# Border to the feed-forward part: operands made product by product, the cross output's second half by rows, the last transposes behind products

## The chip, the core and the metric

One core of a Trainium2 chip runs the kernel. The metric is the device time of one execution in microseconds (us): 1808.42 as the median of three runs (1808.24 to 1808.46). The engines are TensorE (PE), VectorE (DVE), ScalarE (ACT) and GpSimd (POOL); SyncE (SP) issues the transfers. Each engine runs its own instructions in a fixed order and waits where an operand or a buffer is not ready.

## The reference

One layer on 1024 tokens of width 1024, all in float32: an attention part, a cross attention to 256 memory tokens, and a gated feed-forward part. The change touches the seam between the last two:

```
x = x + memory_cross_attention(hc, mn, w_cq, w_ckv, w_co)   # ends in o @ w_co
hf = rmsnorm(x, norm_ffn_g)
g, u = split(hf @ w_gate_up, 2)                             # width 2 x 2816
x = x + (silu(g) * u) @ w_down
out = rmsnorm(x, norm_final_g)
```

## The kernel before

**Three matmuls for one product.** Every float32 operand is split in two halves: `hi` is a cast on ScalarE, `lo = src - hi` a subtraction on VectorE. A product is hi*hi + lo*hi + hi*lo, so three matmuls (`prod`, L887 to L889 in the feed-forward part). Neither half can be made before the operand is there, and the matmul at L888 needs the weight's `lo`.

**End of the cross attention.** The output weights come as eight units of 512 KB (`unit`, L82), each loaded into one of two `raw` buffers and split into one of three `wsp` buffers. A step (`out_steps`, L626) multiplies one block of 128 rows with two units, twelve matmuls, and VectorE adds the result to the residual `xs` (L632), which frees one of two accumulators. Eight row blocks times two halves of columns (`cc`) make sixteen steps. Four jobs hold them (`last_job`, L795): first the row blocks 0 to 3, `cc` 0 and then 1, then the row blocks 4 to 7, all four for `cc` 0 and then all four for `cc` 1. When a row block has both halves, `rms` normalises it: a square on ScalarE (L106), two small steps on GpSimd (L99, L101), a scaling on VectorE (L108). Then `norms` transposes it on TensorE (L789), and ScalarE and VectorE copy the result to `hq` (L792). The last rows' transposes stand before the first feed-forward product.

**Feed-forward products.** Gate and up are done with a scheme of seven products instead of eight: operands of rows 0 to 3 (`b11`, `b21`) and of rows 4 to 7 (`b12`, `b22`) and differences of them. `T[n]` is the split operand of product kind n, `w` the split weight. The order of the kinds is 1, 2, 6, 5, 7, 3, 4. Kinds 1 and 2 need rows 0 to 3 alone; their operands are made in `mov_early`, all others in `mov_late` (L906), four 1024-wide differences on VectorE, four on GpSimd (L914, L917), ten splits. A tile is two 128-wide column blocks of gate and two of up. The products of the first two tiles are ordered so that kinds 1 and 2 of both come first: products 0 to 3 are kinds 1 and 2 of the first tile (gate, up, gate, up), 4 to 7 those of the second tile, and 8 on the kinds 6, 5, 7, 3, 4 of the first tile. `run` (L1062) makes each weight four products ahead (`AHEAD`), and calls `mov_late` at product 1. For kinds 6 and 3 the weights are differences made on GpSimd (L942 to L946). `down_weights` (L1027) makes differences of the down weights of the same tile on GpSimd, after its first product.

**What sets the order.** A scheduler puts the recorded instructions in an order for each engine; within an engine this order is fixed in the built program. The buffers of the weights `fr` are those of the residual `xs`: the loads of the up weights of the first and the second tile wait until the rows 4, 5 and 6, 7 are stored (L804).

## Time and profile before

| what | value |
|---|---|
| time, median of three runs | 1808.42 us |
| profiled execution, its own time | 1810.3 us |
| span of the profiled execution | 1808.5 us |
| TensorE busy | 1746.3 us, 97% of the span |
| VectorE busy | 1102.1 us, 61% |
| ScalarE busy | 765.9 us, 42% |
| GpSimd busy | 524.5 us, 29% |

TensorE's busy time is an upper view: matmuls overlap and their ends are modelled. What a wait costs is better read from the start of one matmul to the start of the next. In the 40 slices of the span TensorE is at 9 tenths or more in all but four: the first, one in the middle at 7 tenths (the 26th, from about 1130 to 1176 us), the one behind it and the last.

### The profile page before, as it was taken

The page shows a single profiled execution, that of the slowest core. Times are in us where ns is not written, and L with a number is a line of the kernel's source. Part 1 is how long each engine was busy: PE and PEld are TensorE (multiplying, and loading weights), DVE is VectorE, ACT ScalarE, POOL GpSimd, SP SyncE. Part 2 cuts the span into 40 slices and gives each one's busy share as a digit, 9 for nine tenths or more (in the row PEclk, how much of TensorE's full clock was granted, in tenths as well). Part 3 has the DMA queues.
Part 4 walks back from the last instruction along what each step waited for, and adds up shares of the span by engine and source line. Part 5 has one row for each costly group of instructions (what it writes and reads, how often), then busy time and mean ns, then how long its engine had stood idle before and what let it go on. Part 6 is the DMA issues. An engine that isn't in the chain of part 4 may idle for free.

```text
span 1808.5 us, 23594 instructions
## 1 busy us (share of the span) xinstructions
PE 1746.3 (97%) x8836; PEld 1472.0 (81%) x8836; DVE 1102.1 (61%) x1491; ACT 765.9 (42%) x1425; POOL 524.5 (29%) x559
## 2 busy tenths in 40 slices
PE   7999999999999999999999999789999999999996
PEld 7778797898898888888888887578888888888885
DVE  6585667646756644445644546886676656655555
ACT  5354455535545544213542244443333333334343
POOL 3232213213323202200000001676666655400001
PEclk9999999999999999999999999989999999999999
DMA  5332313212222265422421123244445435586663
GB/s 191 105 88 68 103 42 102 70 53 62 78 72 68 82 233 196 151 78 71 140 82 59 47 70 140 93 151 182 180 159 190 163 140 186 205 285 195 191 194 117
DMA packets 75731, 229.81 MB, mean 127 GB/s; under 512 B 9184, under 2 KB 9440, under 8 KB 71776
## 3 DMA queue, kind: packets, MB, share of 16 engines
q1 hardware_dynamic: 75616, 228.30, 37.3%
q8 instruction: 69, 1.13, 0.3%
q14 instruction: 46, 0.38, 0.1%
HBM read 160.10 MB, written 55.57 MB: 119 GB/s over the span
## 4 chain that ended last, share of the span: by engine, by line
PE 66%; DVE 3%; issue 2%; ACT 2%; POOL 1%; DMA 0%; DVEq 0%; POOLq 0%; ACTq 0%
PE bk L888 11%; PE bk L889 11%; PE bk L887 11%; PE acc L215 5%; PE acc L216 5%; PE acc L217 5%; PE s L93 2%; PE s L94 2%; PE s L95 2%; PE s L215 2%; PE s L216 2%; PE s L217 2%; PE av L452 1%; DVE T L882 1%; PE tr L436 1%
## 5 line engine op out<-in xcount | busy, mean ns | idle before, releaser
L215 PE MATMUL acc<-t,wsp 128*128 128x512 f32 (+1 forms) x704 | 270.6, 384 | 0.0
L217 PE MATMUL acc<-t,wsp 128*128 128x512 f32 (+1 forms) x704 | 270.5, 384 | 0.0
L216 PE MATMUL acc<-t,wsp 128*128 128x512 f32 (+1 forms) x704 | 270.4, 384 | 0.0
L888 PE MATMUL bk<-T,w 128*128 128x512 f32 x616 | 241.3, 392 | 14.0 <-DVE w L882 14.0
L887 PE MATMUL bk<-T,w 128*128 128x512 f32 x616 | 241.0, 391 | 0.0
L889 PE MATMUL bk<-T,w 128*128 128x512 f32 x616 | 240.6, 391 | 0.0
L882 DVE TENSOR_TENSOR w<-fr,w 128x512 fp32r<-128x512 f32 x132 | 148.3, 1157 | 70.1 <-ACT w L881 69.8
L79 DVE TENSOR_TENSOR wsp<-raw,wsp 128x1024 fp32r<-128x1024 f32 x100 | 124.6, 1246 | 72.2 <-ACT wsp L74 71.0
L74 ACT CAST wsp<-raw 128x1024 fp32r<-128x1024 f32 x98 | 102.7, 1048 | 126.3 <-PE s L217 50.2
L217 PEld LDWEIGHTS acc<-t,wsp 128*128 128x128 f32 x704 | 133.3, 189 | 25.3
L216 PEld LDWEIGHTS acc<-t,wsp 128*128 128x128 f32 x704 | 133.3, 189 | 23.0 <-DVE wsp L79 0.7
L215 PEld LDWEIGHTS acc<-t,wsp 128*128 128x128 f32 x704 | 133.3, 189 | 22.2
L888 PEld LDWEIGHTS bk<-T,w 128*128 128x128 f32 x616 | 116.5, 189 | 39.5 <-DVE w L882 15.3
L882 DVE TENSOR_TENSOR do<-dr,do 128x1024 fp32r<-128x1024 f32 x77 | 96.8, 1260 | 82.8 <-ACT do L881 82.1
L889 PEld LDWEIGHTS bk<-T,w 128*128 128x128 f32 x616 | 116.5, 189 | 24.2
L887 PEld LDWEIGHTS bk<-T,w 128*128 128x128 f32 x616 | 116.3, 189 | 24.4 <-ACT hq L792 0.2
L881 ACT CAST do<-dr 128x1024 fp32r<-128x1024 f32 x77 | 80.9, 1050 | 118.2 <-PE bk L889 102.9
L215 PE MATMUL acc<-wsp,t 128*128 128x256 f32 (+1 forms) x384 | 124.7, 325 | 1.0 <-POOL wsp L78 1.0
L217 PE MATMUL acc<-wsp,t 128*128 128x256 f32 (+1 forms) x384 | 122.9, 320 | 1.5 <-DVE wsp L79 1.5
L216 PE MATMUL acc<-wsp,t 128*128 128x256 f32 (+1 forms) x384 | 123.0, 321 | 0.0
L888 PE MATMUL bk<-do 128*128 128x512 f32 x308 | 120.2, 390 | 1.3 <-DVE do L882 1.3
L889 PE MATMUL bk<-do 128*128 128x512 f32 x308 | 119.8, 389 | 0.0
(204 smaller groups left out, 3726.2 us busy)
## 6 DMA issues: line engine op xcount, KB each, us to landing
fr<-in_wgu SPq DMA_DIRECT2D x44, 512.0 KB, 5.2
dw<-in_wdn SPq DMA_DIRECT2D x22, 512.0 KB, 5.2
wd<-dw SPq DMA_DIRECT2D x11, 1024.0 KB, 3.9
ad<-r SPq DMA_DIRECT2D x22, 512.0 KB, 3.4
sd<-s SPq DMA_DIRECT2D x11, 1024.0 KB, 4.2
dr<-sd SPq DMA_DIRECT2D x44, 256.0 KB, 3.8
dr<-wd SPq DMA_DIRECT2D x44, 256.0 KB, 4.0
dr<-ad SPq DMA_DIRECT2D x33, 256.0 KB, 5.0
```

Source lines behind the costliest of these rows:

```text
L74: act.copy(out=hi, in_=src)
L79: lo_eng.tensor_tensor(out=lo, in0=src, in1=hi.bitcast(F32), op=ALU.subtract)
L93: pe.matmul(acc, lh, rh, start=(i == 0), stop=False)
L94: pe.matmul(acc, ll, rh, start=False, stop=False)
L215: pe.matmul(acc, lh, rh, start=(i == 0), stop=False)
L216: pe.matmul(acc, ll, rh, start=False, stop=False)
L217: pe.matmul(acc, lh, rl, start=False, stop=(i == n - 1))
L881: self.act.copy(out=hi, in_=src)
L882: self.dve.tensor_tensor(out=lo, in0=src, in1=hi.bitcast(F32), op=ALU.subtract)
L887: mm(acc, l[0], r[0], start=start, stop=False, skip_group_check=onto)
L888: mm(acc, l[1], r[0], start=False, stop=False, skip_group_check=onto)
L889: mm(acc, l[0], r[1], start=False, stop=stop, skip_group_check=onto)
```

## The change

- The second half of the cross output is no longer two jobs. `last_half` takes row block after row block, both halves of columns one after the other, with all four weight units resident: two in `wsp`, two in buffers of `t1`. Each row block is normalised and stored at once.
- `ff.before()` (early operands and the first two weights) stands behind the first step of that half.
- The last row block's transposes (`last_norm`) come behind products 0 and 1, into banks of the feed-forward part.
- `mov_late` is cut in four. The table `LATE` calls it at products 2, 7, 9 and 11 for the kinds 6 (with 5), 7, 3 and 4, and its four differences of GpSimd are VectorE's.
- The down weights of the first two tiles are made in the third and the fourth tile.

```diff
...
 LAM_INIT = 0.2
 AHEAD = 4
+LATE = {2: 6, 7: 7, 9: 3, 11: 4}
 LAG = 1
 F0, FA, FB, W0, W1 = 3, 5.5, 3.8, 0.3, 1.2
...
-    def unit(src, hi_eng=act):
+    def unit(src, hi_eng=act, home=None):
         raw = wp.tile([P, D], F32, name="raw", tag="raw", bufs=2)
         sp.dma_start(out=raw, in_=src)
-        w = wp.tile([P, 2, D], F32R, name="wsp", tag="wsp", bufs=3)
+        w = home([P, 2, D]) if home else wp.tile([P, 2, D], F32R, name="wsp", tag="wsp", bufs=3)
         split(w[:, 0], w[:, 1], raw, hi_eng, dve)
         return w
...
         hq = {}
-        def norms(n):
+        def norms(n, mk=None):
             while len(todo) > n:
                 t, xn = todo.pop(0)
                 half, o = divmod(t, 4)
                 for g in range(2):
-                    ps = (tr_tile if g == 0 else av_tile)()
+                    ps = (mk or (tr_tile if g == 0 else av_tile))()
...
-        def last_job(hh, cc):
+        def last_rms(tt):
+            xn = row_tile()
+            rms(xrow(tt), gbc, xn)
+            if tt % 2:
+                sp.dma_start(out=x_d[tt // 2], in_=xs[tt // 2])
+            todo.append((tt, xn))
+        def last_job(cc):
             def go(w):
-                for tt in range(hh * 4, hh * 4 + 4):
+                for tt in range(4):
                     yield from out_steps(o_sta(2), w, 4, cc, tt)
                     if cc == 1:
                         norms(1)
-                        xn = row_tile()
-                        rms(xrow(tt), gbc, xn)
-                        if tt % 2:
-                            sp.dma_start(out=x_d[tt // 2], in_=xs[tt // 2])
-                        todo.append((tt, xn))
-                    else:
-                        norms(0)
+                        last_rms(tt)
             return Job(Units(wco[4 + cc], wco[6 + cc]), go)
+        def last_half():
+            ws = [[unit(wco[4 + cc + 2 * i], home=t1_tile if cc else None) for i in range(2)] for cc in range(2)]
+            for tt in range(4, 8):
+                add_out(o_sta(2), ws[0], 4, 0, tt)
+                if tt == 4:
+                    norms(0)
+                    ff.before()
+                add_out(o_sta(2), ws[1], 4, 1, tt)
+                norms(0)
+                last_rms(tt)
         for h in range(4):
             u0, u1 = UnitX(h, 0), UnitX(h, 1)
...
                 feed.add(*Q[h + 1, 0])
                 feed.fill(6)
             else:
-                feed.add(last_job(0, 0))
+                feed.add(last_job(0))
                 feed.fill(8)
             u1.t()
             feed.drain()
         gbc = gain_tile(g_ffn)
-        jobs = [last_job(0, 1), last_job(1, 0), last_job(1, 1)]
-        feed.add(*jobs)
-        feed.need(*jobs[:2])
+        feed.add(last_job(1))
...
         ff = FeedForward(tc, tiles, cst, dram, hq, x_d, wgu, wdn, g_final, mhalf, out)
-        ff.before()
         feed.drain()
-        norms(0)
+        last_half()
         psctx.close()
-        ff.run()
+        ff.run(lambda: norms(0, ff.bank))
     ctx.close()
...
         for i in (0, 2):
             self.put(2, i, self.quad(i + 4, 0))
-    def mov_late(self):
-        dve, pool, sub, quad = self.dve, self.pool, ALU.subtract, self.quad
+    def mov_late(self, n):
+        dve, sub, quad = self.dve, ALU.subtract, self.quad
         for i in (0, 2):
-            b11, b12, b22 = quad(i, 0), quad(i, 1), quad(i + 4, 1)
-            dve.tensor_tensor(out=b11, in0=b12, in1=b11, op=sub)
-            self.put(5, i, b11)
-            dve.tensor_tensor(out=b11, in0=b22, in1=b11, op=sub)
-            self.put(6, i, b11)
-            pool.tensor_tensor(out=b12, in0=b22, in1=b12, op=sub)
-        for i in (0, 2):
-            b21 = quad(i + 4, 0)
-            pool.tensor_tensor(out=b21, in0=b21, in1=quad(i, 0), op=sub)
-            self.put(7, i, quad(i, 1))
-        for i in (0, 2):
-            self.put(3, i, quad(i + 4, 1))
-        for i in (0, 2):
-            self.put(4, i, quad(i + 4, 0))
+            b11, b21, b12, b22 = quad(i, 0), quad(i + 4, 0), quad(i, 1), quad(i + 4, 1)
+            if n == 6:
+                dve.tensor_tensor(out=b11, in0=b12, in1=b11, op=sub)
+                self.put(5, i, b11)
+                dve.tensor_tensor(out=b11, in0=b22, in1=b11, op=sub)
+                self.put(6, i, b11)
+            elif n == 7:
+                dve.tensor_tensor(out=b12, in0=b22, in1=b12, op=sub)
+                self.put(7, i, b12)
+            elif n == 3:
+                self.put(3, i, b22)
+            else:
+                dve.tensor_tensor(out=b21, in0=b21, in1=b11, op=sub)
+                self.put(4, i, b21)
     class Pair:
...
     class Tile2:
-        def __init__(self, ff, f):
-            self.ff, self.f = ff, f
+        def __init__(self, ff, f, before=None):
+            self.ff, self.f, self.before = ff, f, before
             self.g, self.u = ff.Pair(ff, f), ff.Pair(ff, FT + f)
             self.w = {}
...
             g, u, ff = self.g, self.u, self.ff
             if p is g:
-                if n == 1:
+                if n == 1 and self.f >= 4:
                     self.down_weights()
                 elif n == 7:
                     act.activation(g.r[1][:, 1], g.r[1][:, 1], AF.Silu)
...
+            elif n == 7 and self.before:
+                self.before.down_weights()
             elif n == 3:
                 pool.tensor_tensor(out=g.r[0], in0=g.r[0], in1=u.r[0], op=ALU.mult)
                 sp.dma_start(out=ff.a_d[self.f // 2][:, 0:2], in_=g.r[0])
...
     def before(self):
-        tiles = [self.Tile2(self, f) for f in range(0, FT, 2)]
+        tiles = []
+        for f in range(0, FT, 2):
+            tiles.append(self.Tile2(self, f, tiles[-2] if f in (4, 6) else None))
         self.items = []
         for ns, ts in ((self.ORDER[:2], tiles[:2]), (self.ORDER[2:], tiles[:2]), (self.ORDER, tiles[2:])):
             for t in ts:
...
         for i in range(2):
             self.make(i)
-    def run(self):
+    def run(self, last_norm):
         with self.tc.tile_pool(name="fps", bufs=1, space=bass.MemoryType.PSUM, reuse_waits="tile") as self.fps:
             later = []
             self.steps = [(n, j) for n in self.ORDER for j in range(FT // 2)]
...
             for i in range(2, AHEAD):
                 self.make(i)
             for i, (t, p, n) in enumerate(self.items):
-                if i == 1:
-                    self.mov_late()
+                if i == 2:
+                    last_norm()
+                if i in LATE:
+                    self.mov_late(LATE[i])
                 self.make(i + AHEAD)
                 if i == len(self.items) - 9:
                     for k in range(4):
```

In the rows of the order `xs` is the residual, `acc` an accumulator, `hq` the transposed rows, `T` a split operand, `w` a split weight from `fr` or `s1`, `r` a partial sum read from bank `bk`; numbers tell buffers apart.

VectorE before, around the early operands (kinds 1 and 2) and the steps of rows 4 to 7:

```order
L792 COPY hq_10350<-av_10437 128x4x128
L882 TENSOR_TENSOR T_10518<-hq_10343,T_10518 128x1024
L632 TENSOR_TENSOR xs_7671<-xs_7671,acc_10443 128x512
L882 TENSOR_TENSOR T_10521<-hq_10343,T_10521 128x1024
L632 TENSOR_TENSOR xs_7673<-xs_7673,acc_10457 128x512
L882 TENSOR_TENSOR T_10524<-hq_10350,T_10524 128x1024
L882 TENSOR_TENSOR T_10527<-hq_10350,T_10527 128x1024
L79 TENSOR_TENSOR wsp_10402<-raw_10400,wsp_10402 128x1024
L632 TENSOR_TENSOR xs_7673<-xs_7673,acc_10471 128x512
```

VectorE after, at the same place:

```order
L794 COPY hq_10373<-av_10470 128x4x128
L895 TENSOR_TENSOR T_10476<-hq_10366,T_10476 128x1024
L895 TENSOR_TENSOR T_10479<-hq_10366,T_10479 128x1024
L895 TENSOR_TENSOR T_10482<-hq_10373,T_10482 128x1024
L895 TENSOR_TENSOR T_10485<-hq_10373,T_10485 128x1024
L634 TENSOR_TENSOR xs_7671<-xs_7671,acc_10505 128x512
L634 TENSOR_TENSOR xs_7671<-xs_7671,acc_10527 128x512
L110 SCALAR_TENSOR_TENSOR xn_10519<-xs_7671,rstd_10524,gbc_10257 128x1024
L634 TENSOR_TENSOR xs_7671<-xs_7671,acc_10541 128x512
```

The two residual adds that stood between the four splits of `T` now stand behind all four.

VectorE before, from the low half of product 5's weight (`w_10696`) to that of product 7 (`w_10777<-fr_10542`), and the split behind it:

```order
L882 TENSOR_TENSOR w_10696<-fr_10542,w_10696 128x512
L912 TENSOR_TENSOR hq_10343<-hq_10618,hq_10343 128x1024
L882 TENSOR_TENSOR w_10777<-fr_10533,w_10777 128x512
L977 TENSOR_TENSOR r_10712<-r_10712,bk_10780 128x512
L882 TENSOR_TENSOR T_10736<-hq_10343,T_10736 128x1024
L882 TENSOR_TENSOR T_10741<-hq_10611,T_10741 128x1024
L882 TENSOR_TENSOR T_10745<-hq_10611,T_10745 128x1024
L882 TENSOR_TENSOR T_10748<-hq_10618,T_10748 128x1024
L882 TENSOR_TENSOR T_10751<-hq_10618,T_10751 128x1024
L882 TENSOR_TENSOR T_10754<-hq_10350,T_10754 128x1024
L882 TENSOR_TENSOR w_10777<-fr_10542,w_10777 128x512
L882 TENSOR_TENSOR T_10757<-hq_10350,T_10757 128x1024
```

VectorE after, from the low half of product 5's weight (`w_10684`), over those of product 6 and 7 (`w_10747`), to the first of product 8 (`w_10780`):

```order
L895 TENSOR_TENSOR w_10684<-fr_10500,w_10684 128x512
L925 TENSOR_TENSOR hq_10366<-hq_10560,hq_10366 128x1024
L895 TENSOR_TENSOR T_10732<-hq_10366,T_10732 128x1024
L895 TENSOR_TENSOR w_10747<-fr_10491,w_10747 128x512
L927 TENSOR_TENSOR hq_10366<-hq_10567,hq_10366 128x1024
L991 TENSOR_TENSOR r_10700<-r_10700,bk_10750 128x512
L895 TENSOR_TENSOR w_10747<-fr_10500,w_10747 128x512
L895 TENSOR_TENSOR T_10736<-hq_10366,T_10736 128x1024
L895 TENSOR_TENSOR T_10740<-hq_10366,T_10740 128x1024
L991 TENSOR_TENSOR r_10717<-r_10717,bk_10766 128x512
L927 TENSOR_TENSOR hq_10366<-hq_10567,hq_10366 128x1024
L895 TENSOR_TENSOR w_10780<-fr_10488,w_10780 128x512
```

Product 7's weight stood behind six splits of `T` after product 6's; now a difference and a read stand between the two, and the differences (L925, L927) and splits of kinds 5 and 6 are spread among the weights.

VectorE after, from the last operand of kind 6 (`T_10744`) over those of kind 7 (`T_10835`, `T_10839`) and 3 (`T_10873`, `T_10876`), with the weights of products 11, 12, 13 and 14:

```order
L895 TENSOR_TENSOR T_10744<-hq_10366,T_10744 128x1024
L930 TENSOR_TENSOR hq_10560<-hq_10567,hq_10560 128x1024 x2
L895 TENSOR_TENSOR w_10818<-s1_10781,w_10818 128x512
L895 TENSOR_TENSOR T_10835<-hq_10560,T_10835 128x1024
L895 TENSOR_TENSOR T_10839<-hq_10560,T_10839 128x1024
L895 TENSOR_TENSOR w_10857<-fr_10488,w_10857 128x512
L895 TENSOR_TENSOR T_10873<-hq_10567,T_10873 128x1024
L895 TENSOR_TENSOR T_10876<-hq_10567,T_10876 128x1024
L895 TENSOR_TENSOR w_10857<-fr_10497,w_10857 128x512
L895 TENSOR_TENSOR w_10894<-fr_10488,w_10894 128x512
```

The weight of product 13 (`w_10857<-fr_10497`) stands behind both operands of kind 3, which product 14 is the first to use; before, all these operands came ahead of product 7's weight.

## Rows read from the trace of the kernel before

**Rows 1.** The page's first line.
```profile
span 1808.5 us, 23594 instructions
```
**Rows 2.** TensorE's waits, 1050 to 1210 us: total us, times, longest.
```profile
PE bk L888 <- DVE w L882: 14.0, 3, 10.8
PE tr L789 <- DVE xn L108: 3.5, 3, 2.0
PE acc L217 <- DVE wsp L79: 1.5, 1, 1.5
PE av L789 <- DVE hq L792: 1.1, 1, 1.1
```
**Rows 3.** Short windows: length, busy us (count) by engine, granted clock, DMA.
```profile
1145.00:1150.00 5.00, 5.00 (x19) 4.03 (x19) 4.88 (x6) 1.76 (x3) 2.02 (x1) 0.71 0.58 213
1160.00:1165.00 5.00, 2.70 (x13) 1.90 (x12) 5.00 (x3) 0.00 (x0) 5.00 (x4) 1.00 0.00 0
1180.00:1185.00 5.00, 3.94 (x9) 3.14 (x10) 5.00 (x6) 0.92 (x2) 4.25 (x3) 0.50 0.00 0
```
**Rows 4.** TensorE's timeline at the border: start, duration, line, operation, idle before.
```profile
1112.55 0.39 PE L216 MATMUL acc<-wsp,t 128*128 128x512 f32 x1
...
1145.87 0.80 PE L887 MATMUL bk<-T,w 128*128 128x512 f32 x1
...
1152.40 0.39 PE L887 MATMUL bk<-T,w 128*128 128x512 f32 x1
...
1160.56 0.39 PE L887 MATMUL bk<-T,w 128*128 128x512 f32 x1
...
1165.87 0.39 PE L887 MATMUL bk<-T,w 128*128 128x512 f32 x1
...
1169.84 0.39 PE L887 MATMUL bk<-T,w 128*128 128x512 f32 x1
1181.06 0.79 PE L888 MATMUL bk<-T,w 128*128 128x512 f32 x1 [10.84 <-DVE w L882]
...
1185.73 0.40 PE L887 MATMUL bk<-T,w 128*128 128x512 f32 x1
```
**Rows 5.** VectorE's timeline at the border.
```profile
1111.95 1.28 DVE L108 SCALAR_TENSOR_TENSOR xn<-xs,rstd,gbc 128x1024 f32<-128x1024 f32 x1 [1.59 <-ACT wsp L74]
...
1117.42 1.28 DVE L108 SCALAR_TENSOR_TENSOR xn<-xs,rstd,gbc 128x1024 f32<-128x1024 f32 x1 [0.71 <-POOL rstd L101]
...
1140.27 0.69 DVE L882 TENSOR_TENSOR w<-fr,w 128x512 fp32r<-128x512 f32 x1
...
1146.69 2.35 DVE L910 TENSOR_TENSOR hq<-hq 128x1024 f32<-128x1024 f32 x2
...
1161.45 1.75 DVE L882 TENSOR_TENSOR w<-fr,w 128x512 fp32r<-128x512 f32 x1
...
1167.64 12.77 DVE L882 TENSOR_TENSOR T<-hq,T 128x1024 fp32r<-128x1024 f32 x6
```
**Rows 6.** ScalarE's timeline at the border.
```profile
1115.06 1.06 ACT L106 ACTIVATE xn<-xs 128x1024 f32<-128x1024 f32 x1 [1.69 <-DVE xs L632]
...
1120.13 3.90 ACT L881 CAST T<-hq 128x1024 fp32r<-128x1024 f32 x4
```
**Rows 7.** GpSimd's timeline at the border, and once beside an idle VectorE.
```profile
1147.98 6.65 POOL L914 TENSOR_TENSOR hq<-hq 128x1024 f32<-128x1024 f32 x2 [5.15 <-DVE hq L910]
...
1158.15 4.49 POOL L942 TENSOR_TENSOR s<-fr 128x512 f32<-128x512 f32 x2
...
1283.62 1.29 POOL L1034 TENSOR_TENSOR dw<-dw 128x512 f32<-128x512 f32 x1 [1.84 <-issue]
```
**Rows 8.** Transfers, 1090 to 1205 us: count, size, median us from issue to landing.
```profile
fr<-in_wgu SPq DMA_DIRECT2D x12, 512.0 KB, 4.1
xd<-xs SPq DMA_DIRECT2D x4, 1024.0 KB, 4.3
```
**Rows 9.** GpSimd's waits, 1200 to 1400 us: total us, times, longest.
```profile
POOL r L1016 <- ACT w L881: 49.6, 6, 11.1
```

## The prediction

> **What bounds the kernel now.** I read the page first: the span is 1808.5 us [rows 1], and its line on TensorE has that engine busy nearly all the time, so time can come only from the places where it stands still. The list of TensorE's waits is next: over the whole program its largest entry belongs to the border to the feed-forward part, where 20.1 us are idle in four groups, 14.0 of them on VectorE's low halves of weights [rows 2]. The table of short windows adds that the granted clock fell there twice, to 0.71 and 0.50 as means of 5 us, the lower of the two levels (1.2 instead of 2.4 GHz) for a part of them, each time after TensorE had stood still [rows 3].
>
> TensorE's timeline gives the price by start times, which is safer than idle figures. A product is twelve matmuls, and three products take 1152.40 to 1160.56, so 2.72 us each and 0.227 per matmul [rows 4]. Number the feed-forward products from 0. Product 0 starts at 1145.87, product 2 at 1152.40, product 5 at 1160.56, 6 at 1165.87, 7 at 1169.84, 8 at 1185.73 [rows 4]. From 2 to 8 that is 33.3 us for 16.3 of work: 17.0 lost. Of these the second matmul of product 7 alone waits 10.84, and the eleven gaps behind it take 4.67 instead of 2.50, 2.2 us for the clock [rows 4]. Why so late is in VectorE's timeline: a row of six splits of T, 12.77 us, stands ahead of that weight's low half [rows 5]. GpSimd works all that time [rows 7]: a step of 1024 columns takes 1.13 in a series without it (two differences in 2.35, one end overlapping) and 2.13 here, a split of 512 takes 0.69 (0.6 in a series) alone and 1.75 beside GpSimd [rows 5].
>
> **The change, part by part.** Number of matmuls, transposes, loads and casts: unchanged. Everything hangs on order. The orders are the same up to the matmul at 1112.55 [rows 4], from where I count both.
>
> *Cross output by rows.* Row block 4's second weight unit is now split behind row 2's norm, a residual add and a copy. The norm starts at 1111.95 and takes 1.28 [rows 5]; so TensorE waits 0.5 for row 2's transposes (1113.3), 0.7 for the copy that frees their second bank (1114.5), 0.9 for the split (1115.65): 2.1 where before 1.5 stood [rows 2]. Next, the early operands: before, residual adds stood between their four splits, now all four are ahead of row 4's last add (the order shows it), and that add frees one of two accumulators. The four casts on ScalarE start when row 3's transposes are copied, 1119.2 by my count, and take 3.90 [rows 6]; the last split ends at 1125.1, the add at 1125.7. TensorE would be there at 1123.15: a new wait of 2.6. Row 4's norm follows its add: 2.36 from the start of the square to that of the scaling (1115.06 to 1117.42) and 1.28 more [rows 5, 6], ready at 1129.5, one product after the add: 1.0 of wait. Rows 5 and 6 have two products behind their last add, 5.4 us against 3.6, and cost nothing; row 7 has products 0 and 1. The three waits for norms (3.5) and the copy (1.1) of before [rows 2], and the slow clock behind them, go. From 1129.5 there remain four cross products (10.9), products 0 and 1 (5.4), four rows of transposes (0.8 each) and some hand-offs: product 2 starts at 1149.3. Before it was 1152.4: 3.1 us won.
>
> *The late operands, one product at a time.* With product 2 at Z = 1149.3, VectorE has this list up to product 8: a copy, four differences and four splits of 1024, six splits of 512, two reads of PSUM. Row 7's copy waits for transposes that now stand behind product 1, and all the rest is queued behind it on VectorE: nothing starts before Z+0.7. Its third entry is a low half of the weights of product 5, which hangs on the last load: row 7's add ends at 1144.3, its store lands 4.3 later, the load that overwrites the buffer another 4.1 or somewhat more [rows 8], the cast 0.6: Z+4.8. From there on each step costs its own time, and GpSimd's eight differences of weights, which now start at 1146.8 right behind row 7's norm, get between. GpSimd's 512-wide difference takes 1.29 with VectorE idle, 2.2 beside it (4.49 for two) [rows 7]; VectorE's 512-wide split grows by 1.1. So I let the two take turns, each VectorE step from SBUF waiting out one of GpSimd's at 1.2 while there are some. The list then runs: product 6's low half at Z+12.4 (needed Z+11.1: 1.35 of wait), product 7's in time, product 8's first weight at Z+19.5 (needed Z+17.9: 1.6) and its second operand at Z+21.9 (0.8 more). Sum 3.75.
>
> Behind it GpSimd gets its buffer for the second tile's eight differences, and the turns begin anew: operands of product 12 (two splits, 2.3 each), its first weight 1.8, two splits for product 14, and only then the weight of product 13. It ends at Z+37.7; product 13 would start at Z+33.9: 3.7 of wait. Small ones at 12, 15 and 16 make 0.9 together. All of it 8.35; before, three waits of 14.0 us idle [rows 2] cost 2.59 + 1.25 + 10.99 = 14.8 by start times [rows 4], 0.28 more each, so with five larger waits I add some 1.2: 9.6 us are lost where 17.0 were.
>
> *Four differences from GpSimd to VectorE.* On GpSimd two took 6.65, on VectorE two take 2.35 [rows 5, 7], so they enter the list above at 1.13 each; GpSimd's list gets shorter by about 12 us, and its weight differences start 11 us earlier (before at 1158.15 [rows 7]).
> The Trainium skill, in "Perfetto Trace Analysis", section "Optimizing Scalar/DVE Operations", says that the two share a read port, so that moving work between them might not help. The rows agree on the contention, but not that the move is neutral: VectorE's own difference is shorter than the turn it would wait. By the page's word alone this part would be worth nothing, some 4 x (2.2 - 1.13) = 4.3 us less, 1802.3.
>
> *Down weights moved to the third and fourth tile.* Four GpSimd differences each, two loads and a store. Here they leave the crowded stretch; there GpSimd waits up to 11.1 us per tile for ScalarE's weights [rows 9], and four differences take 5.2 alone (1.29 each) and up to 9 beside VectorE [rows 7]: cost 0, and if that cover were gone, some 7 us per tile. On SP the fifth tile's weight loads come to stand behind the moved store, which waits for those differences; they are due some ten products (27 us) later, so that costs 0 too.
>
> **Sum.** 3.1 + (17.0 - 9.6) = 10.5 us. The profiled execution took 1810.3 (span 1808.5 and 1.8 around it [rows 1]): 1799.8; it lies 1.9 above the median of the runs, 1808.4, so 1798 there.
>
> Bounds. The unknown is the price of a turn. From below: if VectorE goes first everywhere, at 1.13 and 0.6, the list reaches product 8 in time and no wait is left, 9.6 less: 1788.4. From above: 2.2 per turn (GpSimd's figure beside VectorE) instead of 1.2, on some fourteen turns that count, but half of it covered by the waits already in: 7 us, 1805. I stay at 1.2, the nearest row (0.69 to 1.75).
>
> **Rivals.** *The waits vanish* (0.17): GpSimd's first eight differences run mostly while VectorE stands waiting for row 7 and for the last load, and the rest slips between. For it: VectorE has 3.4 us of idle there by my count. Against it: 17.0 us of the old profile are this very contention. 1789.
>
> *No change that counts* (0.14): TensorE's clock falls again behind the 2.6 and 3.7 us waits, at 2.2 each, and the last load lands 3 us later, which moves product 8 one for one: 10.5 - 4.4 - 3 = 3 us, 1805.3. For it: the clock fell after waits of 1.1 and 2.0 close together [rows 2, 3]. Against it: around product 5, whose wait cost 2.6, it stayed at 1.00 [rows 3, 4].
>
> *Slower* (0.07): the down weights in tiles three and four now make two sets per tile on GpSimd, the new one standing ahead of the differences for the sixth product. If the two sets together outlast GpSimd's 11.1 us of slack, the weights of the next tile come late by a set, 7 us, in both tiles: 14 us against the 10.5, 1812. It decides once less than a set's 7 us of slack is left. Against it: the 11.1 us stood there beside one set already, and TensorE has no wait on weights there.
>
> **How the numbers follow.** The forecast, 1798, has 0.62, with a range of its own from 1793 to 1803 (half a turn more or less). This measurement can tell 0.2%, 3.6 us. Faster: 0.62 + 0.17 and a little of the second rival, 0.80; the same 0.13; slower 0.07. The range takes in the first rival and the second: 1788.5 to 1806.
>
> **What would show it.** In the new profile TensorE's waits at the border should add up to some 14 us instead of 20.1, in about eight pieces, none above 4: one near 2.6 on a residual add behind four splits, one at product 8, one at product 13 for a weight behind two splits of T. Row 7's transposes should come behind product 1 without a wait. VectorE's 1024-wide steps behind them should take 1.1 to 2.4, and GpSimd's first weight difference should start right after the last norm. The down weights should add no TensorE wait in tiles three and four. The forecast is wrong if a single wait over 6 us remains, if the clock shows a stretch at the lower level for more than 5 us, or if the border has no waits at all.

## The result and the profile after

1798.74 us as the median of four runs (1796.97 to 1801.18), against 1808.44 (1808.24 to 1808.77) of the kernel before beside it: a ratio of 0.9947, 95% interval 0.9934 to 0.9959, so 9.7 us faster where 10.5 were forecast. The profiled execution is the longest of the four, 1801.2 us; its span is 9.1 us shorter than that of [rows 1]:
```profile
span 1799.4 us, 23586 instructions
```
TensorE's waits from 1050 to 1210 us (total, times, longest) answer to [rows 2]:
```profile
PE bk L900 <- ACT r L989: 5.0, 2, 2.5
PE acc L217 <- DVE xs L634: 2.5, 1, 2.5
PE bk L901 <- DVE w L895: 1.3, 1, 1.3
PE acc L219 <- DVE wsp L81: 0.7, 1, 0.7
PE av L791 <- DVE hq L794: 0.5, 1, 0.5
PE tr L791 <- ACT t L76: 0.5, 1, 0.5
PE bk L902 <- DVE T L895: 0.5, 1, 0.5
PE bk L900 <- ACT hq L794: 0.2, 1, 0.2
```
11.2 us instead of 20.1, in nine pieces, none above 2.5. The largest entry is one that the forecast did not have: ScalarE's copy of a partial sum. TensorE's timeline shows where the pieces lie (start, duration, idle before):
```profile
1125.97 0.50 PE L217 MATMUL acc<-t,t 128*128 128x512 f32 x1 [2.49 <-DVE xs L634]
...
1149.96 1.03 PE L791 MATMUL bk<-ident,xn 128*128 128x128 f32 x8
1150.75 0.48 PE L900 MATMUL bk<-T,w 128*128 128x512 f32 x1
...
1168.83 0.50 PE L901 MATMUL bk<-T,w 128*128 128x512 f32 x1 [1.27 <-DVE w L895]
1171.17 0.50 PE L902 MATMUL bk<-T,w 128*128 128x512 f32 x1 [0.45 <-DVE T L895]
...
1199.36 0.50 PE L900 MATMUL bk<-T,w 128*128 128x512 f32 x1 [2.52 <-ACT r L989]
...
1204.83 0.50 PE L900 MATMUL bk<-T,w 128*128 128x512 f32 x1 [2.43 <-ACT r L989]
```
Row 7's transposes (1149.96) stand behind product 1 and wait for nothing; product 2 starts at 1150.75; 1168.83 and 1171.17 are in product 8; 1199.36 and 1204.83 are the first matmuls of products 18 and 19. The windows for [rows 3] (granted clock third from the end):
```profile
1125.00:1130.00 5.00, 4.03 (x11) 3.20 (x12) 2.80 (x4) 1.15 (x2) 0.74 (x2) 0.69 0.00 0
1160.00:1165.00 5.00, 5.00 (x24) 4.14 (x23) 5.00 (x5) 2.01 (x3) 1.88 (x2) 1.00 0.00 0
1180.00:1185.00 5.00, 5.00 (x24) 4.14 (x23) 5.00 (x6) 3.35 (x5) 5.00 (x1) 1.00 0.00 0
1205.00:1210.00 5.00, 5.00 (x16) 3.96 (x17) 5.00 (x6) 2.32 (x6) 4.37 (x4) 0.66 0.27 108
```
The two old falls (0.71, 0.50) are gone; there are two new ones, 0.69 behind the wait of 2.49 and 0.66 behind those of 2.52 and 2.43, about 1.6 us each: the eleven gaps behind the waits of 2.49 and 2.43 take 4.12 and 4.21 us instead of 2.50, a part of them at the lower of the two levels (1.2 instead of 2.4 GHz). VectorE's timeline, for [rows 5]:
```profile
1156.72 2.32 DVE L895 TENSOR_TENSOR T<-hq,T 128x1024 fp32r<-128x1024 f32 x1
1158.96 1.77 DVE L895 TENSOR_TENSOR w<-fr,w 128x512 fp32r<-128x512 f32 x1
...
1166.36 0.68 DVE L991 TENSOR_TENSOR r<-r,bk 128x512 f32<-128x512 f32 x1
...
1173.91 2.36 DVE L895 TENSOR_TENSOR T<-hq,T 128x1024 fp32r<-128x1024 f32 x2
...
1185.40 1.29 DVE L895 TENSOR_TENSOR w<-fr,w 128x512 fp32r<-128x512 f32 x2
1186.60 1.28 DVE L991 TENSOR_TENSOR r<-r,bk 128x512 f32<-128x512 f32 x2
```
and GpSimd's, for [rows 7]:
```profile
1146.98 3.52 POOL L956 TENSOR_TENSOR s<-fr 128x512 f32<-128x512 f32 x2
...
1157.92 3.96 POOL L960 TENSOR_TENSOR fr<-fr 128x512 f32<-128x512 f32 x2
1174.13 14.97 POOL L956 TENSOR_TENSOR s<-fr 128x512 f32<-128x512 f32 x2 [12.25 <-ACT w L894]
1189.05 2.54 POOL L957 TENSOR_TENSOR fr<-fr 128x512 f32<-128x512 f32 x2
```
Up to 1162 the two engines take turns as forecast (a step of the one, then a step of the other, each waiting out the step beside it): a T split costs 2.32, a 512-wide split 1.77, GpSimd's differences 1.8 to 2 each. Behind 1163 VectorE's steps are short again (two T splits in 2.36), and GpSimd, which may begin its second tile at 1174.13, needs 14.97 for two differences that take 2.54 elsewhere. The first of them is the longest of its line (ns: least, median, most):
```profile
L956 POOL TENSOR_TENSOR s<-fr x22: 1290/1695/13723, 1147.0 to 1510.2; 128x512 f32<-128x512 f32 x22
```
It ends 1.25 us, a difference's own time, after VectorE goes over to reading PSUM at 1186.60 (L991 adds a bank `bk` of PSUM, where TensorE's products land, to a partial sum; the steps from 1166.96 to there have all their operands in SBUF, the memory of the other buffers here).

From product 24 on every trace below needs 578.4 to 579.9 us, so the kernels differ in the border alone. Each kernel in the table is the kernel after with one edit, told below: u_ takes a part of the change back, i_ and x_ alter a place of it, c_ puts two edits together. Start times count from one and the same matmul, which all kernels share (1050.01 us in the trace after); "16th" is the end of GpSimd's eight differences for the second tile.

| kernel | ratio to before (95%) | product 2 | 8 | 16 | 18 | 24 | 16th |
|---|---|---|---|---|---|---|---|
| before | 1 | 102.1 | 135.4 | 157.2 | 162.7 | 179.0 | 151.4 |
| after | 0.9947 (0.9934-0.9959) | 100.7 | 117.2 | 141.2 | 149.4 | 170.2 | 147.5 |
| u_late | 0.9992 (0.9983-1.0001) | 101.1 | 134.0 | 155.8 | 161.2 | 177.5 | 145.4 |
| u_pool | 0.9973 (0.9962-0.9984) | 100.8 | 118.5 | 150.5 | 155.9 | 172.2 | 147.9 |
| u_down | 0.9970 (0.9958-0.9981) | 100.8 | 117.2 | 141.3 | 154.7 | 173.9 | 147.5 |
| u_norm | 0.9947 (0.9934-0.9959) | 108.4 | 124.7 | 146.5 | 151.9 | 168.4 | 147.3 |
| u_rows | 0.9934 (0.9921-0.9946) | 100.1 | 116.5 | 138.2 | 146.2 | 166.9 | 144.3 |
| i_adds | 0.9931 (0.9918-0.9943) | 98.1 | 114.5 | 138.6 | 146.7 | 167.5 | 144.8 |
| x_slot | 0.9938 (0.9924-0.9951) | 100.7 | 117.1 | 141.2 | 149.5 | 166.0 | 147.4 |
| c_rows | 0.9917 (0.9903-0.9930) | 100.1 | 116.5 | 138.3 | 146.5 | 162.9 | 144.4 |
| i_break | 0.9943 (0.9929-0.9956) | 100.8 | 117.2 | 145.1 | 152.1 | 168.4 | 145.5 |
| c_break | 0.9930 (0.9918-0.9943) | 100.1 | 116.5 | 142.0 | 149.0 | 165.4 | 142.4 |

The kernel before took 1808.8 to 1809.4 beside the experiments, so the ratios compare better than the times; each is known to some 2.3 us. The starts come from one trace per kernel, but where kernels share an order they repeat to 0.1 us: product 2 starts at 100.7 or 100.8 in after, u_pool, u_down, x_slot and i_break, product 8 at 117.1 or 117.2 in four of these. What differs from trace to trace lies outside: the common matmul itself starts at 1048.1 to 1050.4 us. So the starts tell finer differences than the ratios.

### The profile page after: what moved, and what is told of

It is laid out like the page before. It is cut to its first block, busy times and chain, and to the rows that moved or that the text cites. A ratio compares the mean times of both kernels' runs of the same rounds, so it can differ in the third digit from the quotient of the medians.

```text
span 1799.4 us, 23586 instructions
## 1 busy us (share of the span) xinstructions
PE 1745.7 (97%) x8836; PEld 1471.2 (82%) x8836; DVE 1088.5 (60%) x1495; ACT 766.2 (43%) x1425; POOL 519.4 (29%) x555
## 3 DMA queue, kind: packets, MB, share of 16 engines
q8 instruction: 69, 1.13, 0.3%
## 4 chain that ended last, share of the span: by engine, by line
PE 64%; issue 3%; DVE 3%; ACT 1%; POOL 1%; DMA 0%; DVEq 0%; POOLq 0%; ACTq 0%
PE bk L901 11%; PE bk L902 11%; PE bk L900 10%; PE acc L217 5%; PE acc L218 5%; PE acc L219 5%; PE s L95 2%; PE s L96 2%; PE s L97 2%; PE s L217 2%; PE s L219 2%; PE s L218 2%; PE av L454 1%; PE tr L438 1%; PE av L95 0%
## 5 line engine op out<-in xcount | busy, mean ns | idle before, releaser
L895 DVE TENSOR_TENSOR w<-fr,w 128x512 fp32r<-128x512 f32 x132 | 140.8, 1099 | 72.7 <-ACT w L894 72.3
L76 ACT CAST wsp<-raw 128x1024 fp32r<-128x1024 f32 x96 | 100.7, 1049 | 124.5 <-PE s L219 50.2
L901 PE MATMUL bk<-do 128*128 128x512 f32 x308 | 120.2, 390 | 0.8 <-DVE do L895 0.8
L902 PE MATMUL bk<-do 128*128 128x512 f32 x308 | 119.9, 389 | 0.0
L900 PE MATMUL bk<-do 128*128 128x512 f32 x308 | 119.7, 389 | 0.0
L217 PE MATMUL acc<-wsp,t 128*128 128x256 f32 (+1 forms) x368 | 118.1, 321 | 1.1 <-POOL wsp L80 1.1
L219 PE MATMUL acc<-wsp,t 128*128 128x256 f32 (+1 forms) x368 | 116.5, 317 | 0.7 <-DVE wsp L81 0.7
```

What stands on the lines that cost most here:

```text
L76: act.copy(out=hi, in_=src)
L217: pe.matmul(acc, lh, rh, start=(i == 0), stop=False)
L219: pe.matmul(acc, lh, rl, start=False, stop=(i == n - 1))
L895: self.dve.tensor_tensor(out=lo, in0=src, in1=hi.bitcast(F32), op=ALU.subtract)
L900: mm(acc, l[0], r[0], start=start, stop=False, skip_group_check=onto)
L901: mm(acc, l[1], r[0], start=False, stop=False, skip_group_check=onto)
```

## Experiments: which part brought it

**u_late: all late operands ahead of product 2.**
```diff
-                if i in LATE:
-                    self.mov_late(LATE[i])
+                if i == 2:
+                    for k in (6, 7, 3, 4):
+                        self.mov_late(k)
```
Expected: 

> The changed kernel, but all late operands (products 6, 7, 3 and 4 of the seven kinds) are made in one go ahead of product 2. My theory: the low halves of the weights of products 7 and 8 again stand behind ten or more steps on VectorE, one wait of 8 us or more appears there, and the clock falls behind it: 1806 us (1804 to 1809), most of the gain lost. Rival (what counted was taking four differences from GpSimd, not the order): VectorE runs the list without contention and TensorE waits less than 4 us for it: 1799 to 1801.

Measured 1807.64 us, 0.9992: the whole gain is lost. TensorE's waits, 1050 to 1225 us:
```profile
PE bk L901 <- DVE w L895: 9.6, 2, 6.2
...
PE bk L900 <- ACT T L894: 2.3, 1, 2.3
```
Between products 2 and 8 it needs 32.9 us where the kernel after needs 16.4 and the one before 33.3. The size is as my theory had it, though the wait is split in three, the longest 6.2, and the granted clock is 0.62 to 0.70 in the windows of 5 us from 1165 to 1185. Without the order product by product nothing of the gain is left.

**u_pool: the differences of kinds 7 and 4 on GpSimd again.**
```diff
-                dve.tensor_tensor(out=b12, in0=b22, in1=b12, op=sub)
+                self.pool.tensor_tensor(out=b12, in0=b22, in1=b12, op=sub)
...
-                dve.tensor_tensor(out=b21, in0=b21, in1=b11, op=sub)
+                self.pool.tensor_tensor(out=b21, in0=b21, in1=b11, op=sub)
```
Expected: 

> The changed kernel, but the four differences of 1024 columns for kinds 7 and 4 are on GpSimd again, each just ahead of the splits that need it. My theory (VectorE's own step is cheaper than the wait for GpSimd's): VectorE waits for each pair, 2 to 3.5 us longer than its own 1.13 each; GpSimd stood idle for 12 us ahead of the second tile, which hides some: 1801 us (1800 to 1804). Rival (the move is neutral, the two engines share what bounds them): 1799, no difference that can be told. Second rival: GpSimd is locked out by VectorE's chain for 10 us also here, and TensorE gets one wait over 5 us at product 12 or 16: over 1805.

Measured 1803.63 us, 0.9973: 0.26%, 4.7 us, more than the kernel after. One wait of 5.9 us appears, in product 8, for a weight's low half; some of it is made good later, and product 24 starts 2.1 us later than in the kernel after. TensorE's waits, 1050 to 1225 us, and one difference on GpSimd:
```profile
PE bk L901 <- DVE w L895: 7.7, 3, 5.9
...
1164.69 2.84 POOL L930 TENSOR_TENSOR hq<-hq 128x1024 f32<-128x1024 f32 x1
```
The move is not neutral: a difference costs 1.13 in VectorE's series and 2.77 to 3.32 on GpSimd here.

**u_down: the down weights of the first two tiles in their own tiles again.**
```diff
-                if n == 1 and self.f >= 4:
+                if n == 1:
...
-            tiles.append(self.Tile2(self, f, tiles[-2] if f in (4, 6) else None))
+            tiles.append(self.Tile2(self, f, None))
```
Expected: 

> The changed kernel, but the down weights of the first two tiles are made in their own tiles again: four more differences of 512 columns per tile on GpSimd inside the border, two loads and a store. My theory: GpSimd is the late engine there since VectorE's chain keeps it waiting; four differences (5.2 us alone, up to 9 beside VectorE) ahead of the second tile's multiply make products 18 and 19 wait 4 to 9 us longer: 1804 us (1801 to 1808). Rival: GpSimd stood idle for 12.25 us there, which hides them: 1799, no difference.

Measured 1804.24 us, 0.9970. The wait at product 18 grows to 7.8 us (TensorE's waits, 1050 to 1225 us):
```profile
PE bk L900 <- ACT r L989: 8.5, 2, 7.8
```
Four differences of 1.26 stand on GpSimd between the 16th difference and the multiply that ScalarE's copy waits for. GpSimd's idle 12.25 us lie ahead of them and hide nothing.

**u_norm: row 7's transposes ahead of product 0.**
```diff
         last_half()
+        norms(0)
         psctx.close()
-        ff.run(lambda: norms(0, ff.bank))
+        ff.run(lambda: None)
```
Expected: 

> The changed kernel, but row 7's transposes stand ahead of product 0 as before. My theory: TensorE waits for row 7's norm (3.6 us after its add, less the 0.8 us of row 6's transposes), some 2 to 2.5 us, but VectorE's copy and with it the whole list of late operands come two products earlier relative to product 2, so product 8's waits (1.7 us) go: net 0 to 2 us, 1799 to 1801. Rival: the list does not hang on that copy at all, then the 2.5 us wait is lost in full and the clock falls behind it: 1802 or more.

Measured 1799.41 us, 0.9947, no difference by the ratios. TensorE waits 5.25 us for the norm, more than I said, and product 2 starts 7.7 later; yet product 24 starts 1.7 us earlier, since no wait is left at 8, 18 and 19. The later start of product 2 does not set the end of the border: GpSimd's first difference starts at 97.0 in both kernels and its 16th ends at 147.3 and 147.5.

**u_rows: cross output in four jobs again.**
```diff
...
-        feed.add(last_job(1))
+        jobs = [last_job(0, 1), last_job(1, 0), last_job(1, 1)]
+        feed.add(*jobs)
+        feed.need(*jobs[:2])
...
+        ff.before()
         feed.drain()
-        last_half()
+        norms(1)
```
Expected: 

> The changed kernel, but cross output in four jobs as before; row 7's transposes still behind product 1, late operands still product by product. My theory: most of the 9.7 us comes from the late operands; in the changed trace product 2 starts 1.35 us earlier than before, and that is all that the rows bring, so 1800 us (1799 to 1802), with the waits on norms (some 3 us in three pieces) back ahead of product 0 and the 2.49 us wait on the residual add gone. Rival 1: the rows bring the 3.1 us that the prediction gave them: 1802 or more. Rival 2: the list on VectorE hangs on row 7's norm, so what the rows bring there comes back threefold behind product 2: over 1804.

Measured 1796.27 us, 0.9934: not slower at all. Product 2 starts 0.66 earlier without the rows, not 1.35 later, and product 24 3.2 earlier, so all three theories fell. GpSimd's timeline in it:
```profile
1140.08 0.55 POOL L103 TENSOR_TENSOR rstd<-ms,mhalf 128x1 f32<-128x1 f32 x1
1140.60 3.51 POOL L945 TENSOR_TENSOR s<-fr 128x512 f32<-128x512 f32 x2
```
Row 7's norm, behind which GpSimd's differences stand, is done 4.4 us earlier (92.5 against 97.0 on the table's clock), and the 16th difference and products 16, 18 and 24 follow by 3.0 to 3.2. The intervals of the ratios overlap; c_rows below repeats the sign on x_slot (162.9 against 166.0). This edit takes back two things at once, the output by rows and the place of the early operands ahead of row 4's last add; the next one changes the second alone.

**i_adds: the early operands written behind row 4's last add.**
```diff
                 if tt == 4:
                     norms(0)
-                    ff.before()
                 add_out(o_sta(2), ws[1], 4, 1, tt)
+                if tt == 4:
+                    ff.before()
```
Expected: 

> The changed kernel, but the early operands of the feed-forward part are written behind row 4's last residual add, so that on VectorE the add stands ahead of three of the four splits of T. My theory: the 2.49 us wait on that add goes, and with it the slow clock behind it (1.5 us), less up to 1 us for row 4's norm: 1795.5 us (1794 to 1797). Rival 1: three splits now stand ahead of row 4's norm and its transposes wait 2 us and more, nothing won: 1798 to 1800. Rival 2: what is won ahead of product 2 is waited for again at products 8 and 18, since the last load and GpSimd set those: 1798.

Measured 1796.90 us, 0.9931. The wait of 2.49 is gone and the clock stays at 1.00 there; instead row 4's transposes wait 1.51 for the norm:
```profile
1126.10 0.66 PE L791 MATMUL tr<-ident,xn 128*128 128x128 f32 x4 [1.51 <-DVE xn L110]
```
Product 2 and all that follows come 2.6 us earlier, GpSimd's 16th difference too, so nothing is waited for again. By the trace both rivals fell; the intervals of the ratios overlap. Product 24 is at 167.5, against 170.2 in the kernel after and 166.9 in u_rows: of the 3.2 us that u_rows won, 2.6 come back by the place of the early operands alone, and some 0.6 are left for the rows.

## Experiments: the waits at products 18 and 19

**x_slot: buffers of their own for the second tile's first partial sums.**
```diff
+                if self.f == 2:
+                    ff.pair = ff.tiles["four"]("rr")
+                k = 2 * (self.f // FT)
-                self.r = [ff.tiles["sum" if self.f >= FT else "row"]("r"), None]
+                self.r = [ff.pair[:, k:k + 2] if self.f % FT == 2 else
+                          ff.tiles["sum" if self.f >= FT else "row"]("r"), None]
```
Expected: 

> The changed kernel, but the second tile's partial sums of its first product lie in buffers of their own, so ScalarE's copies of them do not wait until GpSimd's two multiplies of the first tile have read theirs. My theory: the waits of 2.52 and 2.43 us at products 18 and 19 go, and the slow clock behind them (1.6 us): 1792.5 us (1791 to 1795). Rival (GpSimd's stand still for 13.7 us beside VectorE's chain is what is late, not the buffers): its three differences for the second tile end at the same time, so product 18 waits for the low half of its weight instead: 1797 to 1799.

Measured 1797.36 us, 0.9938: the rival's number, and the intervals of the ratios overlap; the trace shows more. The wait at product 19 is gone with the slow clock behind it (product 24 at 166.0 instead of 170.2), that at product 18 is still there, with no slow clock behind it (the eleven gaps behind it take 2.64 us):
```profile
1199.10 0.50 PE L900 MATMUL bk<-T,w 128*128 128x512 f32 x1 [2.68 <-ACT rr L993]
...
1201.74 0.39 PE L902 MATMUL bk<-T,w 128*128 128x512 f32 x1
```
In the trace ScalarE's copies, no longer short of a buffer, now stand behind a SiLU that waits for VectorE's sums, and these stand behind the low half of a weight that GpSimd delivers late. So the wait at product 19 was the buffer's, and that at product 18 stays with GpSimd's late differences.

**probe: the two engines alone.** Expected: 

> Not the layer: only differences of float32 tiles from SBUF, in four stages, 5 of 512 columns on GpSimd and 6 of 1024 on VectorE; its output is no part of the reference's. Stage 1: each engine alone. Stage 2: VectorE's chain first, GpSimd joins behind its second step. Stage 3: GpSimd first, VectorE joins behind GpSimd's first. Stage 4: as stage 2, but each VectorE step waits for a cast on ScalarE. Theory A (VectorE's unbroken chain locks GpSimd out): in stage 2 GpSimd's first difference ends only when VectorE's chain ends, 4 to 5 us instead of 1.29, VectorE's steps keep 1.13; in stage 3 VectorE's first step waits out one of GpSimd's and then GpSimd stands; in stage 4 GpSimd gets in between. Theory B (turns, as the prediction had it): in stages 2 and 3 both engines' steps take some 2.1 to 2.4 us. Theory C (both slow down by a share, no lock): both stretch by the same factor in stages 2 to 4.

VectorE's second stage and GpSimd's first difference in it:
```profile
23.92 10.09 DVE L26 TENSOR_TENSOR w<-g,b 128x1024 f32<-128x1024 f32 x6 [0.68 <-ACT g L32]
```
```profile
26.36 2.17 POOL L29 TENSOR_TENSOR q<-w,d 128x512 f32<-128x512 f32 x1 [11.23 <-DVE w L26]
```
Turns: VectorE's steps grow from 1.15 to 2.28, GpSimd's from 1.26 to 2.24, here and in the other two stages with both. Theory A fell in this form: a chain two steps old does not keep GpSimd out. In the kernel GpSimd had done nothing for 12.25 us when it asked, and VectorE's chain was 7.2 us and eight steps old, counted from its read of PSUM at 1166.36.

**probe2: the age of the chain.** Expected: 

> Not the layer: six stages of 1024-column float32 differences on VectorE, unbroken, 9 steps more once GpSimd joins with three of 512 columns; its output is no part of the reference's. GpSimd joins after 3 steps (stage 1) or 14 (stages 2 to 6); in stage 3 a one-column memset and in stage 4 a read of PSUM stand on VectorE four steps behind that point; in stage 5 each VectorE step takes a ScalarE cast made just ahead of it and writes the rounded type, as the splits of T do; in stage 6 GpSimd's output buffer was read before by ScalarE and VectorE. The first probe showed turns (2.2 us a step) where GpSimd joined after 2 steps. Theory A (a chain that has run long without GpSimd keeps it out): stage 1 takes turns at once; in stage 2 GpSimd's first difference lasts the whole rest, 9 to 11 us, and in stages 3 and 4 it gets in at the break, 4 to 6 us. Theory B (the kind of VectorE step decides): turns in stages 1 to 4, GpSimd kept out in stage 5 alone. Theory C (neither, what kept it out in the kernel is something else): turns in all six, 2.2 us for GpSimd's first.

GpSimd's first difference in each of the six stages, in their order:
```profile
9.05 2.10 POOL L39 TENSOR_TENSOR q<-m,d 128x512 f32<-128x512 f32 x1 [8.61 <-DMA d<-in_x]
...
39.06 11.26 POOL L39 TENSOR_TENSOR q<-m,d 128x512 f32<-128x512 f32 x1 [23.50 <-DVE m L36]
...
70.03 5.58 POOL L39 TENSOR_TENSOR q<-m,d 128x512 f32<-128x512 f32 x1 [17.27 <-DVE m L36]
...
100.11 5.58 POOL L39 TENSOR_TENSOR q<-m,d 128x512 f32<-128x512 f32 x1 [20.10 <-DVE m L36]
...
131.27 11.26 POOL L39 TENSOR_TENSOR q<-m,d 128x512 f32<-128x512 f32 x1 [21.18 <-DVE m L36]
...
163.72 11.19 POOL L39 TENSOR_TENSOR q<-m,d 128x512 f32<-128x512 f32 x1 [16.77 <-DVE m L36]
```
VectorE in the second stage, and the memset in the third:
```profile
38.90 10.30 DVE L36 TENSOR_TENSOR o<-g,b 128x1024 f32<-128x1024 f32 x9
...
74.44 0.06 DVE L62 MEMSET tick<- 128x1 f32 x1
```
Theory A in all six. Behind 3 steps GpSimd gets its turn; behind 14 it waits until VectorE's nine further steps, at full speed, are over; a memset of one column (0.06 us) or one read of PSUM lets it in. The Trainium skill, in "SBUF — State Buffer", section "Who interferes with whom", says that a VectorE instruction with two SBUF inputs contends with a GpSimd instruction that reads SBUF, and that one with at most one SBUF input, outside the two-port modes, does not; the two breaks agree with it (5.58 instead of 11.26).

**i_break: such a memset in the kernel.**
```diff
...
-        self.split(t[:, 0], t[:, 1], src)
+        self.split(t[:, 0], t[:, 1], src, n == 3)
...
             else:
-                dve.tensor_tensor(out=b21, in0=b21, in1=b11, op=sub)
+                if i == 0:
+                    self.tc.keep_in_program_order(dve.memset(self.tick, 0.0))
+                self.tc.keep_in_program_order(dve.tensor_tensor(out=b21, in0=b21, in1=b11, op=sub))
```
The last argument of `split` pins kind 3's low halves, and the two differences are pinned too. So VectorE's order changes a little beside the memset: the second difference now stands behind the first split of its kind, where the kernel after has both differences first.
Expected: 

> The changed kernel with a one-column memset on VectorE ahead of the differences of the last kind (it stands 6 us behind the point where GpSimd asks for its second tile); the steps of that kind are pinned in the order difference, split, difference, split. My theory (a break lets GpSimd in, as in the probe; from there the two take turns, and the time that both together need stays the same): GpSimd's first difference of the second tile lasts 7.5 us instead of 13.7, but VectorE's seven steps behind it grow by 1.1 each, GpSimd's last difference ends at most 2 us earlier, part of the waits at products 18 and 19 moves to product 16: 1797 to 1800 us. Rival (being kept out is what costs the 5 us): these waits go and nothing takes their place: 1793 to 1795.

Measured 1799.35 us, 0.9943, no difference by the ratios. GpSimd's timeline, then TensorE's waits, 1050 to 1225 us:
```profile
1174.26 9.59 POOL L962 TENSOR_TENSOR s<-fr 128x512 f32<-128x512 f32 x2 [12.25 <-ACT w L896]
```
```profile
PE bk L904 <- DVE r L997: 3.6, 1, 3.6
PE acc L217 <- DVE xs L634: 2.5, 1, 2.5
```
Its first difference gets in at the memset (two in 9.59 instead of 14.97), VectorE's next steps grow to 2.3, the 16th difference ends 2.0 us earlier. The waits at 18 and 19 are gone, and one of 3.6 stands at the first matmul of product 16, for a read of PSUM that stands on VectorE behind the grown steps, with a slow clock behind it (0.67 as the mean of 1195 to 1200). The time is my theory's: being kept out costs little in sum, it mainly says who is late. By the trace product 24 still starts 1.8 us earlier than in the kernel after.

## Experiments: the best of both

**c_rows: u_rows and x_slot together.** The edit is the sum of the two above. Expected: 

> The changed kernel with cross output in four jobs as before, and with buffers of their own for the second tile's first partial sums. Each of the two alone gave 0.9934 and 0.9938 of the time before, the changed kernel 0.9947. My theory (they act at different places, ahead of product 2 and at products 18 and 19, so they add up): 0.9925 of the time before, 1795.5 us (1794 to 1797). Rival (what comes earlier ahead of product 2 is waited for at product 18, where GpSimd's late differences set the pace): 0.9934 to 0.9938, 1797.

Measured 1794.17 us (1792.58 to 1795.46), 0.9917: the fastest here, below both kernels, and 0.3% below the kernel after. The parts add up; 2.7 us are still lost ahead of product 18 (8.2 us from product 16 to 18 where two products take 5.4).

**c_break: c_rows with the memset.** Expected: 

> The last kernel (cross output in four jobs, buffers of their own for the second tile's first partial sums), with the same memset. There 3.0 us are lost ahead of product 18, which follows GpSimd's differences by 2.1 us, and none between products 2 and 16. My theory (turns or not, the sum of both engines' steps decides): within 1 us of the 1794.2 without it. Rival (being kept out costs): the 3.0 us go: 1791.

Measured 1796.94 us, 0.9930: rather slower than c_rows (the fastest execution, 1795.49, is just above the slowest of c_rows, 1795.46; the intervals of the ratios overlap). GpSimd is done 2.0 us earlier, but product 16 starts 3.7 later, and product 24 2.4. Turns were the worse order here; my "within 1 us" was too narrow, the rival's gain did not come.

## Why the prediction was right, and where not

**The time and its main source: right, the closeness in part luck.** 10.5 us were forecast, 9.7 came. By the traces product 24 starts 8.8 us earlier: 1.4 of it is won ahead of product 2, where the forecast had 3.1, and 7.5 behind it, where it had 7.4. From product 2 to 20, 9.5 us are lost (18 products take from 100.7 to 159.2 on the table's clock, 58.5, less 18 x 2.72 = 49.0), where the forecast had 9.6, all of it up to product 16. That these two agree is luck: 2.4 us are lost up to product 16, the other 7.1 at products 18 and 19, where the forecast had no wait.

**Ahead of product 2: the waits right, what they are worth wrong.** The waits of 0.5, 0.7 and 0.9 measured 0.48, 0.48 and 0.70, the 2.6 on the residual add 2.49, and rows 5 to 7 cost nothing. Product 2 came 1.4 us earlier instead of 3.1: behind the 2.49 the clock fell (1.6 us), which the sum had left to a rival. It hid the wait of 1.0 for row 4's norm; i_adds brought that out at 1.51. The rest of the difference, some 1.1 us, lies in the add, 0.5 later than counted, and in small hand-offs. What won at product 2 was not the output by rows: it starts at 102.1 before, at 100.1 where of the changes ahead of it only row 7's transposes are moved (u_rows), at 108.4 with the rest of the change and the transposes not moved (u_norm). And by u_rows and i_adds the new order ahead of product 0 took some 3 us of the border rather than bringing any, 2.6 of them by early operands that stand ahead of row 4's last add. The forecast had GpSimd's list start right behind row 7's norm, but priced no delay of that norm.

**Up to product 8: right.** The turns cost what [rows 5] gave (1.75 there, 1.77 here; 2.32 for a step of 1024). Product 6's 1.35 did not come; product 8's 1.6 and 0.8 came as 1.27 and 0.45. One reading was loose: in the profile before, GpSimd did not work through all of VectorE's six splits but stood for their last 2.2 of 12.77 us (its step ends at 1178.19), which changes no term of the sum.

**Behind product 8: the step that failed.** "The turns begin anew" for the second tile. They did not: VectorE's chain kept GpSimd out, so VectorE's operands were early and product 13's 3.7 never came. GpSimd's results were late instead, and with the buffer that its multiply frees they made the 2.52 and 2.43 at products 18 and 19. That being kept out mainly moves the lateness from one engine to the other is shown by i_break (same time within what the ratios tell, other wait). That the cause is one resource of both engines is what the probes suggest; that the whole border is as long as this resource is busy was not measured.

**Four differences on VectorE: right in sign, the size open.** They were said to be worth 4.3 us; u_pool lost 4.7 by the ratios (each known to some 2.3 us) and 2.1 in the trace.

**Down weights: right that they cost nothing where they went** (no new wait of TensorE behind 1210), but their leaving is worth about 4 us (u_down: 0.23%, 3.7 in the trace), which the forecast did not count apart.

**The rivals.** Slower: refuted. No change: half of it came. The clock fell twice, at 1.6 each instead of 2.2: once behind the wait on the residual add, as this rival had it, and once behind the waits at products 18 and 19 instead of one at 13. The load was in time. The waits vanish: refuted.

## What to carry to other kernels

Where VectorE and GpSimd both read pairs of operands from SBUF, add up both lists before moving steps between them or in their order. Here another order changed mainly whose consumer waits (i_break: same time by the ratios), and once it cost 2.4 us (c_break); that the sum alone sets the time is not shown. When a step is moved ahead of the products, look what it does to the start of the longest list behind them: here early operands ahead of a residual add delayed the last norm, and GpSimd's list behind it, by 2.7 us (i_adds). A wait of 2.5 us on TensorE can bring a slow clock with it (1.6 us behind the one of 2.49), but need not (none behind x_slot's 2.68): price it as a range.

## What the runs showed of the hardware

A VectorE chain of differences and splits, both inputs in SBUF, without a gap or a break, kept GpSimd out until it ended: 13.72 us for a difference that takes 1.29 in the kernel, 11.26 in the probe. It needs some age: with 2 or 3 steps behind it GpSimd got its turn, with 14 (some 16 us) not. In u_pool GpSimd asked 5.3 us after its own last step and took turns:
```profile
1181.78 3.85 POOL L956 TENSOR_TENSOR s<-fr 128x512 f32<-128x512 f32 x2 [5.29 <-issue]
```
In u_norm it asked when the chain behind VectorE's last read of PSUM was 6.0 us and seven whole steps old (1170.85 to 1176.84), and was kept out, 10.29 us for the first of two differences:
```profile
1176.84 11.54 POOL L957 TENSOR_TENSOR s<-fr 128x512 f32<-128x512 f32 x2 [14.53 <-DVE w L896]
```
If a read of PSUM and a turn of GpSimd both start the count anew, the limit lies between some 5 and 6 us of chain; if only GpSimd's own steps do, between 5.3 and 12.25. Which of the two, and whether it counts time or steps, was not tried.
